# Attention's queries as seven-product units in a stage of their own, ahead of attention, in a hybrid encoder block

## The chip, the cores and the metric

One core of a Trainium2 chip runs the whole layer. The metric is the device time of one execution in microseconds. Engines are named as in the profile: TensorE (PE, with its weight loads PEld), VectorE (DVE), ScalarE (ACT), GpSimd (POOL), and SyncE (SP), whose queue issues nearly all the transfers.

## The reference

One encoder layer on 16 learned meta tokens followed by 1024 tokens of width 1024. `u` is the normed stream; one projection of it feeds everything:

```python
z = u @ w_in
rq, rk, rv, rg, aq, ak, av, ag, gr, ga = _split_in(z)
# retention: 4 heads, keys of 128, values of 256, rotary on rq and rk, scanned forward and backward
o_r = _bidirectional_retention(rq, rk, rv, lg_f, lg_b)[:, META_PAD:]   # then group norm per head
o_r = o_r * ret_nw * silu(rg);            y_r = o_r @ w_rb
# attention: 8 query heads, 2 groups of keys and values, rotary on aq and ak, window of +-128,
# the meta keys always visible, a learned sink logit per head
o_a = _windowed_sink_attention(aq, ak, av, sink)
o_a = o_a * silu(ag);                     y_a = o_a @ w_ab
mix = sigmoid(gr) * y_r + sigmoid(ga) * y_a
return h + _rms_norm(mix @ w_o, post_w)   # meta tokens dropped at the end
```

## The kernel before, in words

**Precision.** Every large product is made from two parts of each operand, a rounded high part (fp32r) and the low rest: `mm3` issues three matmuls, high x high, low x high, high x low. The high part is made by ScalarE (or by GpSimd, `pool_hi`), the low part by VectorE (`dve_lo`, a subtraction). `x`, scaled by the norm's weight and split so, stays in the tiles `big` (two parts of two halves of k); the row factor of the norm is applied behind the products.

**Weights.** `w_in` lies in units of 256 columns: 0 to 3 queries and keys of retention (`U_QK`), 4 to 7 its values, 8 to 11 its gates, 12 and 13 attention's keys and values (`U_AK`, `U_AV`), 14 to 17 its queries (`U_AQ`), 18 to 21 its gates, 22 to 29 the merge gates.

**Order of the work.**

1. Setup: loads, `x` in parts, the first head's queries and keys.
2. Retention, head by head (`retention(h, fill)`): values are projected and the chunks run forward; then a second pass runs the chunks backward. Between its short matmuls `fill` advances a generator of other work: the next head's queries and keys (`gen_qk`) and some early gate products, and for the last head attention's keys (`gen_ak`) and the first two query units (`gen_aq`), 16 steps a chunk.
3. Attention's values (`gen_av`), kept in SBUF as `vah` and `val`.
4. `attention()`: 32 chunks, each of 64 tokens and the four heads of one key group, in three stages (scores and softmax; transposes; values). A chunk's three stages lie apart in time, and between them `fill` advances `works`: the other two query units, then the early gate products. `START` and `FILL` say how much, in units of half a step; a step is one `mm3` of 128x512. `BEGUN` says at which step other things start: fetches, splits, and the sums of `x` (`sum_fetch`, `sum_scale`, `sum_row`), which go to DRAM as `xs`.
5. `steps`, from `run(phases)`: phase "z" (all 16 gate units), "r" and "a" (the two branch projections, 4 units each) and "o" (the output projection).

**Seven products.** A unit in a `Phase` is a product of 256 x 1024 by 1024 x 1024, cut into 2 x 2 blocks and made from seven block products instead of eight, of sums of blocks: operands A11, A12, S4, A22, S1, S2, S3 against B11, B21, B22, T4, T1, T2, T3 (`PROD`). One block product is 12 matmuls of 128x512. `prepare` makes a weight operand's sum and its two parts, `LEAD` = 6 products ahead; `product` issues the matmuls; `combine` adds up in PSUM banks X, Y, Z and in SBUF; `post` finishes an output. T1 to T4 are sums of blocks of `x`. Products that need only plain `x` can be made early (`PRE`, `gen_pre`): they go to DRAM as `e` and are added later.

The query projection, in contrast, is plain: `proj` runs 8 blocks of k, 3 matmuls each, for each of two column halves and two token halves, 96 matmuls a unit (`paq`), and `rope_evac` turns the result from PSUM: three multiplications on VectorE and an addition on GpSimd.

The order in which each engine issues is the program's order as a scheduler arranges it; `tc.issue_after` and `follow` pin some instructions behind others.

Of the kernel before, what the change touches and what calls it, by code (L numbers as in the profile page):

```python
# [14 lines left out]
NM = 16  # L15
T = NM + SEQ
P = 128
# [9 lines left out]
START = 6, 6  # L27
FILL = (((5, 4),) * 1 + ((5, 5),) * 1 + ((6, 4),) * 1 + ((4, 3),) * 1 + ((4, 5),) * 2 + ((4, 7),) * 1 + ((3,
        5),) * 1 + ((6, 4),) * 1 + ((5, 4),) * 1 + ((5, 3),) * 1 + ((2, 4),) * 1 + ((5, 7),) * 1 + ((4, 5),)
        * 1 + ((1, 4),) * 1 + ((6, 1),) * 1 + ((3, 5),) * 1 + ((4, 5),) * 1 + ((4, 4),) * 1 + ((6, 4),) * 1 +  # L30
        ((4, 4),) * 1 + ((4, 3),) * 1 + ((3, 4),) * 1 + ((4, 4),) * 1 + ((4, 2),) * 1 + ((4, 4),) * 1 + ((5,
        4),) * 1 + ((3, 4),) * 1 + ((4, 4),) * 1)
PRE = {u: (2, 3) if u > 4 else (2,) for u in range(2, 14)}
# [11 lines left out]
def block_kernel(ctx: ExitStack, tc: tile.TileContext, xT, x, meta, w_in, w_rb, w_ab, w_out, vecs, dec, sink,  # L45
# [25 lines left out]
    xs_d = [dram.tile([4, P, 2, 512], F32, tag=f"xs{i}", name=f"xs{i}") for i in range(2)]  # L71
# [3 lines left out]
    latest = []  # L75
# [76 lines left out]
    xm = wp.tile([P, KT, 2 * 32], R, tag="xm", bufs=1, name="xm")  # L152
    nc.vector.memset(xm.bitcast(F32), 0.0)

# [25 lines left out]

    ra_stack = ExitStack()
    ra = ra_stack.enter_context(tc.tile_pool(name="ra", bufs=1, reuse_waits="tile"))
    ident = ra.tile([P, P], F32, name="ident")
    cr = ra.tile([P, T], F32, name="cr")
    sr = ra.tile([P, T], F32, name="sr")
# [12 lines left out]
    DT = ra.tile([P, NH, P], F32, tag="DT", bufs=1, name="DT")  # L198
    tabt = ra.tile([P, MW], F32, tag="tab", bufs=1, name="tabt")
    idx = tabt[:, 3 * P:3 * P + 5]  # L200
    warm = ra.tile([P, 1], F32, name="warm")
    dect, neg, na, e, e2, s_, ss, acc, lg = (ra.tile([P, 8], F32, name=n) for n in (
        "dect", "neg", "na", "e", "e2", "s_", "ss", "acc", "lg"))
    ecst, ex = (ra.tile([P, 28], F32, name=n) for n in ("ecst", "ex"))
# [40 lines left out]
    def decay_table(hs):  # L245
        for h in hs:
            t = ra.tile([P, P], F32, tag="rw", bufs=3, name=f"dd{h}")
# [158 lines left out]
    def row_factors(cs):  # L406
# [3 lines left out]
        for c in cs:  # L410
            a, b = cols(c)
            n = b - a
            rw = ra.tile([P, P], F32, tag="rw", bufs=3, name=f"rw{c}")
            nc.scalar.copy(rw[0:n], rcol[0:n, c:c + 1].to_broadcast([n, P]))
            nc.tensor.transpose(t[:, a - base:b - base], rw[0:n], ident[0:n, 0:n])
# [25 lines left out]
    vah = va.tile([P, NB, 256], R, name="vah")  # L441
    vm = va.tile([NM, 2, 256], R, name="vm")
# [4 lines left out]
    rp = r_stack.enter_context(tc.tile_pool(name="rp", bufs=1, reuse_waits="tile"))  # L447

# [16 lines left out]
    pend, masks = [], []  # L465

    def retention(h, fill):
        q, kt = qk[h]
# [9 lines left out]
        vmeta = rp.tile([NM, 256], F32, tag="vmeta", bufs=2, name=f"vmeta{h}")  # L478
# [14 lines left out]
        def stage1(c):  # L493
            n = NM if c == 0 else P
            pv = first.pop(0) if first else projT(wv, c, f"pv{h}_{c}", vmeta)
            vh = rp.tile([P, 256], R, tag="vh", bufs=4, name=f"vh{h}_{c}")
            vl = rp.tile([P, 256], R, tag="vl", bufs=4, name=f"vl{h}_{c}")
# [7 lines left out]
            for d in ("f", "b"):  # L505
# [3 lines left out]
                a = rp.tile([P, P], R, tag="kh" + d, bufs=2, name=f"kh{d}{h}_{c}")  # L509
                b = rp.tile([P, P], R, tag="kl" + d, bufs=2, name=f"kl{d}{h}_{c}")  # L510
# [5 lines left out]
            if c > 0:  # L516
                sd = rp.tile([P, P], F32, tag="sd", bufs=3, name=f"sd{h}_{c}")
                a = rp.tile([P, P], R, tag="sh", bufs=3, name=f"sh{h}_{c}")
                b = rp.tile([P, P], R, tag="sl", bufs=3, name=f"sl{h}_{c}")
# [44 lines left out]
        for c in range(9):  # L564
# [7 lines left out]
            if h == NH - 1 and c == 1:  # L572
                wak.append(load_w(w_in, U_AK))
                masks.append(ra.tile([P, MW], F32, tag="tab", bufs=1, name="mask"))
                nc.sync.dma_start(masks[0], tab[:, 0:MW])
# [10 lines left out]


# [21 lines left out]
        for c in range(NB, 0, -1):  # L609
# [25 lines left out]
            if c < 8:  # L635
                with ExitStack() as behind:
                    for p in pins:
                        behind.enter_context(tc.issue_after(p))
                    fill(KT if h < NH - 1 else 2 * KT)
            if c < NB - 1:  # L640
                finish(c + 2)
        state["n", 1]()
# [17 lines left out]
    aqf, aqs, wq, made = {}, {}, {}, set()  # L660
    aq_d = [dram.tile([4, P, SEQ], F32, tag=f"aq{g}", name=f"aq_d{g}") for g in range(2)]

    def load_q(g, m):

        assert {(2 * g + p, m // 4, e_) for p in range(2) for e_ in range(2)} <= made
        aqf[g, m] = o = aw.tile([P, 4, P], F32, tag="qf", bufs=2, name=f"qf{g}_{m}")
        nc.sync.dma_start(o, aq_d[g][:, :, P * m:P * m + P].rearrange("h p t -> p h t"))

    def split_q(g, m):

        o = aqf.pop((g, m)).rearrange("p e (b t) -> p b e t", b=2)
        h, l = (aw.tile([P, 2, 4, 64], R, tag=f"aq{t}", bufs=2, name=f"aq{t}{g}_{m}") for t in "hl")
# [4 lines left out]
    def fetch_aq(hp):  # L677
        raw = fetch_w(w_in, U_AQ + hp)
        split, wq[hp] = halves_w(U_AQ + hp)
        begun["q", hp] = lambda s: split(raw[s], "apart")  # L680

    def half_w(which, i, s):
        if (which, i, s) in low_w:
            low_w.pop((which, i, s))()
        else:
            low_w[which, i, s] = begun[which, i](s)

    begun, low_w = {}, {}

    def gen_aq(hp, i):  # L690
        if hp not in wq:
            wq[hp] = load_w(w_in, U_AQ + hp)
        a, b = HALVES[i]
        for e_ in range(2):
            t = yield from proj(wq[hp], P * e_, a, b, f"paq{hp}_{i}{e_}")
            o = ra.tile([P, 512], F32, tag="q", bufs=6, name=f"aq{hp}_{i}{e_}")
            with follow(*marks("lo")):
                rope_evac(t, a, b, o, f"aq{hp}_{i}{e_}")
            made.add((hp, i, e_))
            nc.sync.dma_start(aq_d[hp // 2][2 * (hp % 2) + e_, :, 512 * i:512 * i + 512], o)  # L700
            yield

# [3 lines left out]
    ak_d = dram.tile([P, T], F32, tag="ak", name="ak_d")  # L706
    later_k = []

    def load_k():

        later_k.append(aw.tile([P, T], F32, tag="kf", bufs=1, name="kf"))
        nc.sync.dma_start(later_k[0], ak_d)

    def keys(g, i, x, meta=None):

        if not i:
            kT[g] = [ra.tile([P, NB, 144], R, tag="kp", bufs=2, name=f"kT{s}{g}") for s in "hl"]
# [11 lines left out]
    def gen_ak(g, pieces_=range(4)):  # L729
        if not wak:  # L730
            wak.append(load_w(w_in, U_AK))
        for i in pieces_:
# [4 lines left out]
            if g:  # L737
                nc.sync.dma_start(ak_d[:, a:b], o[:, 0:b - a])
            else:
                s = NM if i == 0 else 0  # L740
                keys(g, i, o[:, s:s + 256], None if i else o[:, 0:NM])
# [5 lines left out]
    def sum_fetch(q):  # L747

        k, c = q // 2, slice(256 * (q % 2), 256 * (q % 2) + 256)
        xsum[q] = {}  # L750
        for i in range(2):
            xsum[q][i] = t = xs_tile[q % 2][i](f"xs{i}{q}")
            nc.sync.dma_start(t, xT[4 * i + k, :, NM:T].rearrange("p (j t) -> p j t", j=2)[:, :, c])

    xs_tile = [(lambda n, tag=tag: aw.tile([P, 2, 256], F32, tag="xs", bufs=2, name=n)) for tag in range(2)], [
        lambda n: ra.tile([P, 2, 256], F32, tag="DT", bufs=1, name=n),
        lambda n: wp.tile([P, 2, 256], F32, tag="xm", bufs=1, name=n)]

    def sum_scale(q):

        for i, t in xsum[q].items():
            nc.scalar.activation(t, t, AF.Copy, scale=vec[:, 4 * i + q // 2:4 * i + q // 2 + 1])

    def sum_row(q):

# [890 lines left out]
```

## Time and profile before

| | |
|---|---|
| three runs | 1059.12, 1059.22, 1060.39 us (median 1059.22) |
| profiled execution | 1059.64 us, of which the span from first to last instruction is 1057.8 us |
| granted TensorE clock | 0.998 |
| busy: PE / DVE / ACT / POOL | 98% / 80% / 46% / 20% |
| DMA | 191.67 MB, mean 181 GB/s |
| attention's key projection | 271 to 304 us |
| value projection | 352 to 377 us |
| attention, first scores to last value product | 379 to 564 us |

How to read it: stretches are in microseconds from the span's start. Groups give line, engine, operation, output and inputs by the program's names, shape and count, then busy time, mean length of one in ns, and the engine's idle time just before them with what ended it. Matmuls overlap, so their lengths add up to more than the time they take.

### The profile page before, as it was taken

The numbers are of one execution on the slowest core, as the hardware profiler recorded it, in microseconds if no ns is written. First come the engines' busy times: TensorE is split into PE (matmuls) and PEld (weight loads), VectorE is DVE, ScalarE is ACT, GpSimd is POOL, SyncE is SP. The second block draws the span as 40 slices with busy tenths as digits, with TensorE's granted clock in tenths as the row PEclk, the third lists the DMA queues.
The fourth block names the chain that finished last, engine by engine and source line by source line (L and its number), as shares of the span: only waits on it lengthen the run. The fifth ranks groups of instructions, "written<-read, shape, count | busy, mean of one in ns | idle before, by whom it ended". The sixth has DMA issues, their size and how long they took to land.

```text
span 1057.8 us, 17121 instructions
## 1 busy us (share of the span) xinstructions
PE 1039.7 (98%) x5845; PEld 899.5 (85%) x5845; DVE 850.9 (80%) x1753; ACT 485.9 (46%) x1068; POOL 216.5 (20%) x272
## 2 busy tenths in 40 slices
PE   8999999999999999999999999999999999999996
PEld 7998999989998988978987888777888888787885
DVE  7887788778988458797869988999799799768664
ACT  5541432413411245566667444455466455343442
POOL 3425225325244124322210000000000000111032
PEclk9999999999999999999999999999999999999999
DMA  9412312303123626577759779999925747789365
GB/s 332 160 60 86 106 59 90 125 12 129 51 81 100 189 83 193 165 239 213 209 161 313 216 245 324 305 334 340 373 90 180 256 142 262 196 230 326 91 99 80
DMA packets 110551, 191.67 MB, mean 181 GB/s; under 512 B 11056, under 2 KB 49840, under 8 KB 109632
## 3 DMA queue, kind: packets, MB, share of 16 engines
q1 hardware_dynamic: 106576, 183.49, 52.5%
q0 software_dynamic: 3744, 6.82, 4.4%
q8 instruction: 46, 0.75, 0.3%
q14 instruction: 41, 0.34, 0.1%
q10 hardware_dynamic: 144, 0.27, 0.1%
HBM read 128.67 MB, written 63.18 MB: 181 GB/s over the span
## 4 chain that ended last, share of the span: by engine, by line
PE 81%; DVE 8%; DMA 6%; ACT 2%; issue 2%; SPq 0%; DVEq 0%; POOLq 0%; ACTq 0%
PE bz L80 5%; PE bz L79 5%; PE bz L81 5%; PE pv L81 3%; PE pv L79 3%; PE pv L80 3%; PE paq L80 3%; PE paq L79 3%; PE paq L81 3%; PE bo L80 2%; PE bo L79 2%; PE bo L81 2%; PE ba L80 2%; PE ba L79 2%; PE ba L81 2%
## 5 line engine op out<-in xcount | busy, mean ns | idle before, releaser
L1242 POOL DMA_DIRECT2D mx_d<-c1a x4 | 3.7, 917 | 394.8 <-DVE c1a L1233 391.5
L79 PE MATMUL bz<-T,lhz 128*128 128x512 f32 x192 | 75.6, 395 | 0.5 <-DVE u2z L1026 0.4
L81 PE MATMUL bz<-T,lhz 128*128 128x512 f32 x192 | 75.8, 395 | 0.0
L80 PE MATMUL bz<-T,llz 128*128 128x512 f32 x192 | 75.7, 395 | 0.0
L81 PE MATMUL pv<-wl,big 128*128 128x256 f32 x256 | 73.1, 285 | 0.0
L79 PE MATMUL pv<-wh,big 128*128 128x256 f32 x256 | 72.8, 285 | 0.0
L80 PE MATMUL pv<-wh,big 128*128 128x256 f32 x256 | 72.7, 284 | 0.0
L79 PE MATMUL bz<-big,lhz 128*128 128x512 f32 x172 | 67.8, 397 | 2.0 <-ACT lhz L941 2.0
L80 PE MATMUL bz<-big,llz 128*128 128x512 f32 x172 | 68.2, 396 | 0.0
L81 PE MATMUL bz<-big,lhz 128*128 128x512 f32 x172 | 67.7, 394 | 0.0
L1413 POOL TENSOR_SCALAR p<-p,den 128x352 f32<-128x352 f32 (+2 forms) x60 | 38.9, 661 | 96.7 <-DVE den L1406 86.2
L1403 ACT ACTIVATE p<-raw,nm 128x353 f32<-128x353 f32 (+2 forms) x64 | 36.1, 566 | 43.8 <-DVE nm L1400 41.8
L79 PE MATMUL paq<-big,wh 128*128 128x512 f32 x128 | 51.9, 405 | 0.0
L80 PE MATMUL paq<-big,wl 128*128 128x512 f32 x128 | 50.8, 396 | 0.0
L81 PE MATMUL paq<-big,wh 128*128 128x512 f32 x128 | 50.4, 394 | 0.0
L599 ACT ACTIVATE ost<-to,rnw 128x128 f32<-128x128 f32 x64 | 19.8, 363 | 65.0 <-PE to L594 50.1
L81 PEld LDWEIGHTS pv<-wl,big 128*128 128x128 f32 x256 | 48.3, 189 | 0.4
L79 PEld LDWEIGHTS pv<-wh,big 128*128 128x128 f32 x256 | 48.3, 189 | 0.2
L80 PEld LDWEIGHTS pv<-wh,big 128*128 128x128 f32 x256 | 48.2, 188 | 0.0
L79 PEld LDWEIGHTS bz<-T,lhz 128*128 128x128 f32 x192 | 36.1, 188 | 9.5 <-DVE u2z L1026 1.2
L81 PEld LDWEIGHTS bz<-T,lhz 128*128 128x128 f32 x192 | 36.2, 188 | 8.5
L80 PEld LDWEIGHTS bz<-T,llz 128*128 128x128 f32 x192 | 36.2, 188 | 8.3
(612 smaller groups left out, 3567.6 us busy)
## 6 DMA issues: line engine op xcount, KB each, us to landing
wrz<-in_w_in_dram SPq DMA_DIRECT2D x32, 512.0 KB, 6.2
wr<-in_w_in_dram SPq DMA_DIRECT2D x27, 512.0 KB, 4.0
e<-e SPq DMA_DIRECT2D x42, 256.0 KB, 4.3
we<-in_w_in_dram SPq DMA_DIRECT2D x18, 512.0 KB, 4.1
tg<-tg_d SPq DMA_DIRECT2D x32, 256.0 KB, 4.9
T<-preT SPq DMA_DIRECT2D x6, 1024.0 KB, 7.8
xt<-in_x_dram SPq DMA_DIRECT2D x8, 512.0 KB, 8.8
oTr_d<-ost SPq DMA_DIRECT2D x16, 256.0 KB, 2.2
```

The lines of the kernel that those rows point to most:

```text
L79: nc.tensor.matmul(o, ah, bh, start=first, stop=False, **kw)
L80: nc.tensor.matmul(o, al, bh, start=False, stop=False, **kw)
L81: latest[:] = [nc.tensor.matmul(o, ah, bl, start=False, stop=last, **kw).ins]
L599: nc.scalar.activation(ost[0][:, e_, w0:w0 + P], to[:, P * e_:P * e_ + P], AF.Copy, scale=rnw[:, 2 * h + e_:2 * h + e_ + 1])
L1242: nc.gpsimd.dma_start(d, to, accum_op=ALU.add)
L1403: last["exp"] = nc.scalar.activation(p[:, 0:1 + wid], raw[e_][:, 0:1 + wid], AF.Exp, scale=-1.0, bias=nm_[:, e_:e_ + 1], accum_out=den[:, ...
L1413: nc.gpsimd.tensor_scalar(pt[e_][:, 0:wid], pt[e_][:, 0:wid], den[:, e_:e_ + 1], 1.0, op0=ALU.mult, op1=ALU.mult)
```

## The change: what it does

- **Queries as units of seven products.** The four query units (16 to 19 in the new numbering of gates) leave `gen_aq` and run in a phase of their own, "y", with the gate units 0 to 3 (`FIRST`): eight units, two at a time, after the value projection and before attention. A query's output is turned by `query_post` and stored to `aq_d`. The operands of two units share tiles of the weight pool (`paired`), and operand sums are made in place.
- **Sums of x earlier.** Rows of `x` are loaded and scaled in the last head's second pass and summed during the value projection (`x_load`, `x_scale`, `x_sums`). T1 stays in `big`; T2, T3 and T4 are split for the new phase, written to DRAM in both parts (`t_store`) and read back for phase "z" without a split (`get_sum`).
- **The last head's second pass** advances 9 steps a chunk (`LAST`), the two key groups alone. Both go through DRAM (`ak_d`), as do the values (`av_d`, `vm_d`): attention loads them when it begins.
- **Early products.** Units 4 to 7 and 10 to 15 (`LATER`) now have three, 2, 3 and 5; units 8 and 9 (`EARLY`) none. Product 2 of six units is made in retention (`BORDER`), of the others during phase "y"; 3 and 5 fill attention. Sum S2 goes through DRAM (`s2_d`).
- **Phase "z"** has units 8 and 9 and the ten of `LATER`, these with four products each, 1, 6, 7 and 4. As B21, B22 and T1 are not needed there by then, their refill for the next phase starts 48 products ahead (`REFILL`).
- The sums of `w_out` for phase "o" (`pre_load`, `pre_split`) move from phase "z" into phase "y" and attention.
- Tables (`VALUES_AT`, `FIRST_AT`, `BEGUN`) say at which step each of these is issued. The host lays the units of `w_in` out in blocks.

```diff
-START = 6, 6
-FILL = (((5, 4),) * 1 + ((5, 5),) * 1 + ((6, 4),) * 1 + ((4, 3),) * 1 + ((4, 5),) * 2 + ((4, 7),) * 1 + ((3,
...
-PRE = {u: (2, 3) if u > 4 else (2,) for u in range(2, 14)}
+START = 4, 12
+FILL = ((2, 2),) * 1 + ((2, 1),) * 1 + ((2, 3),) * 2 + ((4, 3),) * 1 + ((2, 3),) * 6 + ((2, 4),) * 1 + ...
+EARLY = 8, 9
+LATER = 4, 10, 5, 11, 6, 12, 7, 13, 14, 15
+PRE = {u: (2, 3, 5) for u in LATER}
+BORDER = 12, 0, 12
+LAST = 9
+REFILL = -48, 5, 5
+LEADS = 2, 4, 6
+VALUES_AT = ((-1, "w1", "s0", "s1"), (1, "l2"), (4, "w0"), (6, "c2"), (8, "n6", "s2", "pT2.0.1.2"),
+             (16, "f0", "l3"), (17, "f1", "f2"), (20, "c3", "z"), (21, "s3", "f3"), (22, "pT2.3"))
+FIRST_AT = ((1, "k6"), (2, "pT3"), (6, "pT4"), (7, "m4"), (12, "tT3"), (13, "x0"), (14, "tT2", "tT4"),
+            (16, "y0.0"), (17, "y0.1"), (18, "y0.2"), (19, "y0.3", "x1"), (23, "y1.0"), (24, "m4", "y1.1"),
+            (26, "y1.2"), (27, "y1.3", "n8"), (28, "x2"), (31, "y2.0", "k8"), (33, "y2.1"), (35, "y2.2"),
+            (37, "y2.3"), (44, "A0"), (47, "m4"), (49, "r", "F4"), (51, "S4", "P4", "A1"),
+            (52, "L4", "F10", "A2"), (53, "A3"), (54, "m4", "S10", "P10", "L10", "F5"))
...
-                    fill(KT if h < NH - 1 else 2 * KT)
+                    fill(KT if h < NH - 1 else LAST)
             if c < NB - 1:
                 finish(c + 2)
+            if h == NH - 1:
+                for f, k in {6: [(x_load, 0)], 5: [(x_load, 1)], 4: [(x_scale, 0)], 3: [(x_scale, 1)]}.get(c, ()):
+                    f(k)
...
-        fill, drain = filler([gen_qk(h + 1), pieces(pre, (8, 8, 4)[h])] if h < 3 else [gen_ak(0), gen_ak(1), gen_aq(0, 0), gen_aq(0, 1), gen_aq(1, 0), gen_aq(1, 1)])
+        fill, drain = filler([gen_qk(h + 1), pieces(pre, BORDER[h])] if h < 3 else [gen_ak(0), gen_ak(1)])
...
         def split(self, u, p, src):
-            h, l = (lp.tile([P, 4, P], R, tag=t, bufs=LEAD, name=f"{t}{self.nm}{u}_{p}") for t in ("lh", "ll"))
+            if self.paired:
+                n, e_ = self.at[u]
+                if not e_:
+                    self.pair[n, p] = [wp.tile([P, 4, 256], R, tag=f"w{x}", bufs=4, name=f"w{x}{self.nm}{n}_{p}")
+                                       for x in "hl"]
+                h, l = (part(t, e_) for t in (self.pair.pop if e_ else self.pair.get)((n, p)))
+            else:
+                h, l = (lp.tile([P, 4, P], R, tag=t, bufs=LEAD, name=f"{t}{self.nm}{u}_{p}") for t in ("lh", "ll"))
             nc.scalar.copy(h, src)
             dve_lo(l, src, h)
...
     def get_sum(n):
-        for k in range(4):
-            t = stage(f"x{n}{k}", n in ("T2", "T3"))
-            i, j = next(o for m, o, *_ in SUMS if m == n)
-            nc.sync.dma_start(t, xs_d[i][k][:, j])
-            split_b(n, k, t)
+        for v, d in zip(B[n], t_d[n]):
+            nc.sync.dma_start(v.bitcast(F32), d)
...
+    def query_post(u, i, j, o, to=None):
+        s, to = half[j], o if to is None else to
+        m2 = spare[0].tile([P, 512], F32, tag="m2", bufs=2, name=f"m2_aq{u}{i}{j}")
+        nc.vector.tensor_tensor(m2[64:128], o[0:64], sr[0:64, s], mul)
+        nc.vector.tensor_tensor(m2[0:64], o[64:128], sr[64:128, s], mul)
+        nc.vector.tensor_tensor(to, o, cr[:, s], mul)
+        nc.gpsimd.tensor_tensor(to, to, m2, add)
+        made.add((u, j, i))
+        nc.sync.dma_start(aq_d[u // 2][2 * (u % 2) + i, :, 512 * j:512 * j + 512], to)
...
+    FIRST = 0, 1, 16, 17, 18, 19, 2, 3
+    first_seq = sequence(FIRST)
+    first_seq[:14] = [(u, p) for u in (0, 1) for p in (1, 2)] + [(u, p) for p in (5, 6, 7, 3, 4) for u in (0, 1)]
+    first_seq[-14:] = [(u, p) for p in (1, 5, 6, 7, 4, 2, 3) for u in FIRST[-2:]]
+    first_phase = Phase("y", first_seq, w_loader(w_in, gates), first_post, first_fetch, paired=True)
+    steps = run([(Phase("z", sequence(EARLY + LATER, (1, 3, 2, 5, 6, 7, 4)), pre_loader, z_post, z_fetch,
+                        early=EARLY, pre=PRE),
...
-        works = hooked([(gen_aq(2, 0), 2), (gen_aq(3, 0), 2), (gen_aq(2, 1), 2), (gen_aq(3, 1), 2), (pre, 2)], BEGUN)
+        works = hooked([(fifths(), 2)], BEGUN)
...
+        nc.sync.dma_start(vah.bitcast(F32), av_d[0])
+        nc.sync.dma_start(val.bitcast(F32), av_d[1])
         edge_values(0, 0)
         edge_values(0, 1)
...
+    jobs = dict(l=x_load, c=x_scale, s=x_sums, p=x_parts, f=x_first, t=t_store, m=more, n=second_fetch,
+                k=second_parts, x=lambda k: pre_load(k, act_src(w_out)), y=pre_split, A=ready, F=pre_fetch, S=pre_sums,
+                P=pre_parts, L=pre_low, z=lambda _: next(first), w=first_weights, r=lambda _: first_phase.raw.clear())
...
+    for n, _ in enumerate(gen_av()):
+        with tc.high_priority(400):
+            do(table, n)
...
+    e_from[0] = p2
+    free[:] = ["pj"] * 3 + ["p1"] * 2 + ["p3"]
+    table = at(FIRST_AT)
+    for n, _ in enumerate(first):
+        do(table, n)
...
+    at1, at2, atv = (a_stack.enter_context(tc.tile_pool(name=n, bufs=1, reuse_waits="tile"))
+                     for n in ("at1", "at2", "atv"))
+    vah, val = (atv.tile([P, NB, 256], R, name=n) for n in ("vah", "val"))
```

In a table, a letter is a job of `jobs`, and what follows it its arguments: "y1.2" makes `pre_split(1, 2)`, "m4" four steps of the early products, "A0" to "A3" ready attention's inputs.

More of the change, by code (lines that the diff above doesn't have):

```diff
@@ new lines, in second_fetch, with second_parts @@
+    def second_fetch(n):
+        pool, tag, bufs = (lp, "w2", 1) if lp else (keep, "wr", 2)
+        fetched_w[n, 2] = t = pool.tile([P, 4, 256], F32, tag=tag, bufs=bufs, name=f"w2_{n}")
+        for i, u in enumerate(LATER[n:n + 2]):
+            nc.sync.dma_start(part(t, i), part(w_in[gates[u], :, 4:8, :], 0))
+    def second_parts(n):
+        h, l, low = parts_of(fetched_w.pop((n, 2)), f"w2_{n}")
+        low()
+        for i, u in enumerate(LATER[n:n + 2]):
+            parts[u, 2] = part(h, i), part(l, i)
@@ L866, in pieces @@
             yield next(gen)
[L868 to L872 removed]
+    pre = seconds()
     softmax, last = [], {}
@@ L1082, in sequence @@
     def sequence(n, first=ORDER):
+        if not isinstance(n, int):
+            return [(u, p) for i in range(0, len(n), 2) for p in (ORDER if i else first) for u in n[i:i + 2]]
         if n % 2:
@@ new lines, in block_kernel, with first_weights @@
+    first = run([(first_phase, None)], {}, lead=lambda i: LEADS[(i > 0) + (i > 2)])
+    def first_weights(u):
+        for n in ("A11", "A12"):
+            first_phase.block(u, n)
+    jobs = dict(l=x_load, c=x_scale, s=x_sums, p=x_parts, f=x_first, t=t_store, m=more, n=second_fetch, k=second_parts, x=lambda k: pre_load(k, act_src(w_out)), y=pre_split, A=ready, F=pre_fetch, S=pre_sums, P=pre_parts,
+                L=pre_low, z=lambda _: next(first), w=first_weights, r=lambda _: first_phase.raw.clear())
```

651 lines of the change are left out of this document (391 added, 260 removed).

## The prediction

> **What bounds the kernel now.** I read the page's head and busy times first, then its chain.
>
> ```profile
> span 1057.8 us, 17121 instructions
> PE 1039.7 (98%) x5845; PEld 899.5 (85%) x5845; DVE 850.9 (80%) x1753; ACT 485.9 (46%) x1068; POOL 216.5 (20%) x272
> PE 81%; DVE 8%; DMA 6%; ACT 2%; issue 2%; SPq 0%; DVEq 0%; POOLq 0%; ACTq 0%
> ```
>
> TensorE sets the time: busy 98%, 81% of the chain. So the first question is how many products TensorE has to issue, the second who makes it wait. Next I read TensorE's timeline inside the query projection, because busy time counts overlapping matmuls.
>
> ```profile
> 332.66 0.40 PE L79 MATMUL paq<-big,wh 128*128 128x512 f32 x1
> 332.89 0.40 PE L80 MATMUL paq<-big,wl 128*128 128x512 f32 x1
> ...
> 334.05 0.39 PE L79 MATMUL paq<-big,wh 128*128 128x512 f32 x1
> ```
>
> A record is 0.39 to 0.40 us long, but the next starts after 0.232 us (seven rows, the middle left out: 1.39 us over six steps). This step, not the record, is the price of one 128x512 matmul: a product of a sequence (4 blocks of k, 3 matmuls each) costs 12 x 0.232 = 2.78 us.
>
> The busy times by stage show who is close behind. Columns: stretch, length, then busy us and instructions of PE, weight load, DVE, ACT, POOL; granted clock, DMA share, GB/s.
>
> ```profile
> 352.50:377.20 24.70, 24.70 (x210) 24.51 (x208) 8.85 (x18) 8.13 (x17) 2.33 (x1) 1.00 0.56 171
> 440.00:500.00 60.00, 57.74 (x346) 50.81 (x345) 48.62 (x117) 38.18 (x97) 15.57 (x22) 1.00 0.69 211
> 500.00:551.00 51.00, 50.15 (x314) 45.19 (x313) 35.99 (x90) 35.87 (x94) 11.86 (x18) 1.00 0.62 182
> 577.00:640.00 63.00, 63.00 (x273) 51.04 (x272) 58.20 (x97) 31.24 (x56) 0.00 (x0) 1.00 0.76 245
> 640.00:760.00 120.00, 117.55 (x503) 94.16 (x502) 105.31 (x173) 61.43 (x106) 0.00 (x0) 1.00 0.98 337
> ```
>
> Here 352.5 to 377.2 is the value projection, the next two are the later part of attention, the last two lie in the gates. In attention TensorE loses 2.26 + 0.85 = 3.1 us, in the full gate stretch 2.45 us where the DMA share is 0.98. The gates live with VectorE 58.2 of 63 us busy and lose nothing: a VectorE near 92% is no bound by itself, as operands are split six products ahead.
>
> **What the change removes.** The groups by line count the query products, and one wait:
>
> ```profile
> L79 PE MATMUL paq<-big,wh 128*128 128x512 f32 x128 | 51.9, 405 | 0.0
> L80 PE MATMUL paq<-big,wl 128*128 128x512 f32 x128 | 50.8, 396 | 0.0
> L81 PE MATMUL paq<-big,wh 128*128 128x512 f32 x128 | 50.4, 394 | 0.0
> L80 PE MATMUL pe<-big,wel 128*128 128x512 f32 x84 | 33.6, 400 | 3.1 <-DVE wel L95 3.1
> ```
>
> The four query units take 384 matmuls; seven products each are 4 x 84 = 336. The gates keep 16 x 84 = 1344 in all, early products included. So 48 matmuls go, all of them on the path: 48 x 0.232 = **-11.1 us**. (By record length it would be 19 us, which the timeline forbids.) The Trainium skill's page "TensorE: Matmul & The Clock Gate", Back-to-back issue gap, gives about 0.131 us sustained for 512 columns, by which the gain would be an estimated 6.3 us; the trace's 0.232 us decides.
>
> **What it adds in the eight-unit stage.** TensorE: 8 x 84 matmuls and 48 of early products beside them. VectorE's prices:
>
> ```profile
> 783.87 0.68 DVE L95 TENSOR_TENSOR llz<-wrz,lhz 128x512 fp32r<-128x512 f32 x1
> 784.47 0.68 DVE L1111 TENSOR_TENSOR z<-z,z 128x512 f32<-128x512 f32 x1
> 785.07 0.68 DVE L95 TENSOR_TENSOR llz<-stz14S,lhz 128x512 fp32r<-128x512 f32 x1
> ...
> 457.90 0.69 DVE L192 TENSOR_TENSOR m_aq<-paq,sr 64x512 f32<-64x512 f32 x1
> 458.60 0.69 DVE L193 TENSOR_TENSOR m_aq<-paq,sr 64x512 f32<-64x512 f32 x1
> ```
>
> Start to start, a 128x512 costs 0.60 us and a rotary half 0.70 us. A query unit needs 7 low splits, 4 operand sums and 3 combines (14 x 0.60 = 8.4 us) and four rotated outputs at 2 x 0.70 + 0.60 = 2.0 us: 16.4 us beside 7 x 2.78 = 19.5 us of TensorE. A gate unit swaps the rotation for two operations an output: 13.2 us. During the four query units (65.6 us) the tables also put twelve splits of w_out (a sum and a low part each, 14.4 us) and one weight low part of two such widths (1.2 us): 81.2 us against TensorE's 28 products and one early product, 29 x 2.78 = 80.6 us. VectorE is full there, and GpSimd adds the rotated halves at the same time:
>
> ```profile
> 312.24 1.29 POOL L194 TENSOR_TENSOR aq<-m_aq,m_aq 128x512 f32<-128x512 f32 x1 [1.42 <-DVE m_aq L193]
> ...
> 312.59 1.22 DVE L95 TENSOR_TENSOR Slb<-Sb,Shb 128x256 fp32r<-128x256 f32 x1
> ...
> 447.70 1.54 POOL L194 TENSOR_TENSOR aq<-m_aq,m_aq 128x512 f32<-128x512 f32 x1 [6.20 <-issue]
> ...
> 448.11 0.69 DVE L95 TENSOR_TENSOR pal<-pt,pah 128x512 fp32r<-128x512 f32 x1
> ...
> L95 DVE TENSOR_TENSOR Slf<-Sf,Shf 128x256 fp32r<-128x256 f32 x32 | 15.1, 470 | 0.8 <-POOL Shf L92 0.6
> ```
>
> Beside such an addition the subtraction of two SBUF tiles took 1.22 us where its like takes 0.47, and ended with it; the one that reads PSUM (pal) was not held. So each of the 16 additions costs VectorE about 0.75 us (12 us), at most its own 1.29 us (20.6 us), at least nothing where PSUM reads fall beside it. The Trainium skill's page "SBUF — State Buffer", Who interferes with whom, states this as a rule: an instruction of VectorE with two SBUF inputs and one of GpSimd that reads SBUF exclude each other; the trace agrees (1.22 against 0.47 us).
>
> VectorE then falls 81.2 + 12 - 80.6 = 12.6 us behind. The weight halves have four pair buffers: one in use, one taken by the early products' parts for long stretches, two ahead, worth 4 products or 11.1 us. About 1.5 us reach TensorE; with the shorter lead at the start and the reordered last pair I take **+3** (0 to +20.6, all of it if nothing is ahead). ScalarE at 46% has room for its 7 high splits a unit.
>
> **Changeovers.** Keys and values now go through DRAM: behind the last outputs of the new stage the SP queue waits for that stage's tiles, then loads two 1 MB value tiles; the edge loads and next queries queue behind them.
>
> ```profile
> 379.11 0.26 PE L79 MATMUL ps<-kTh,aqh 128*128 128x208 f32 x1
> ...
> 393.09 0.28 PE L79 MATMUL po<-pah,vah 128*128 128x256 f32 x1
> ...
> 564.17 0.28 PE L81 MATMUL po<-pbl,v 80*128 80x256 f32 x1
> ...
> 578.19 0.39 PE L79 MATMUL bz<-T,lhz 128*128 128x512 f32 x1
> ...
> T<-preT SPq DMA_DIRECT2D x6, 1024.0 KB, 7.8
> ```
>
> The first value product comes 14.0 us after the first scores. Between them the tables now put 19 units of filler, not 25, at half a step of three matmuls (0.35 us) each, and 4 ahead of the first scores: 14.0 - 2.1 + 1.4 = 13.3 us from the end of the new stage. The loads take 7.8 us if they run together and 15.6 us one after the other, behind the last store: 0 to 4 us late. Into the gates, T2, T3 and T4 are six 1 MB loads, once attention's tiles are free; the first is needed 14.0 us after attention's last product, the others 5.6 us apart, and at 6.2 us a pair (2.1 MB at the 337 GB/s above) they land by about 8, 14 and 20 us: in time, unless other loads sit between. In their own stage the gates then move some 45 MB in 54 x 2.78 = 150 us, 300 GB/s of 337. I take **+2** (0 to +8).
>
> **Attention and gates.** Attention loses half of the rope work and all the sums of x; 80 steps of filler remain of 128. Of its 3.1 us of waits, all in front of an early product's low part, I give back **-2** (-3.1 to +2: eight such parts are made there, as before). The last head's second pass has 9 filler steps per chunk instead of 16; the heads before it live with 8. Sums of x move into the value projection, where VectorE is busy 8.85 of 24.7 us. Gates: **0** (-2.5 to +4).
>
> Sum: -11.1 + 3 + 2 - 2 = -8.1 us. The profiled execution took 1059.6 us (span 1057.8), 0.4 above the median of 1059.22, so 1051.1: I say **1051**.
>
> **Rivals.** (1) VectorE becomes the bound in the query units: GpSimd holds it for all 16 additions in full and the operand lead does not cover it, because a product's split is queued behind the rotation of the one before. Then 20.6 us arrive: 1059.2 - 11.1 + 20.6 + 2 - 2 = 1069. It decides against the change from 11 us of waits on. For it: 81.2 of 80.6 us before any hold; against it: the lead, and PSUM readers in between. (2) The changeovers cost their 8 us and the attention gains nothing: 1059.2 - 11.1 + 3 + 8 = 1059, no change. (3) Everything hides and attention's and the gates' waits go: 1059.2 - 11.1 - 3.1 - 2.5 = 1043. That the count of products does not fall I exclude: the sequences spell out each of them.
>
> **How the numbers follow.** Forecast 54%, its own range 1044 to 1057; (1) 28%, with all that a full VectorE may bring; (2) 8%; (3) 10%. A measurement tells about 0.2% (2.1 us) from no change. Faster is forecast and (3): 64%; same is (2): 8%; slower is (1): 28%. The range, 1043 to 1067, takes in (3), (2) and most of (1).
>
> **What would show it.** Right: 48 fewer 128x512 matmuls at an unchanged step of 0.232 us; queries' products named by the new sequence; in its middle VectorE busy in all of a window, with low splits of 1.2 us beside GpSimd's additions, and only some us of TensorE's idle time ended by VectorE; attention's stretch shorter with less waiting. Wrong: a product of that stage regularly late by half a microsecond or more, the first value product waiting for its DMA, or the first T2 product waiting for a load.

## The result

The changed kernel takes **1068.14 us** (median of six runs, 1067.16 to 1071.10), the kernel before beside it 1059.81 us: a ratio of **1.0077, 95% interval 1.0059 to 1.0094**. It is slower, where 1051 us and "faster" were forecast, and 1 us outside the range. The profiled execution took 1067.16 us. From the head of the page of the changed kernel, with its busy times and its chain:

```profile
span 1065.4 us, 17204 instructions
PE 1033.8 (97%) x5797; PEld 893.1 (84%) x5797; DVE 866.9 (81%) x1750; ACT 510.5 (48%) x1116; POOL 214.7 (20%) x268
PE 80%; DVE 9%; DMA 7%; issue 2%; ACT 1%; POOL 1%; SPq 0%; DVEq 0%; POOLq 0%; ACTq 0%
```

TensorE's records fell from 5845 to 5797: the 48 matmuls are gone. Yet the span grew by 7.6 us, so TensorE lost about 19 us elsewhere. The busy times by stage say where to look (columns as in the prediction):

```profile
336.00:516.00 180.00, 171.38 (x737) 137.46 (x736) 157.04 (x235) 71.62 (x131) 27.45 (x20) 0.99 0.65 227
516.00:560.00 44.00, 35.47 (x193) 29.94 (x192) 32.61 (x79) 25.66 (x62) 8.62 (x14) 0.92 0.76 253
560.00:664.00 104.00, 103.16 (x663) 93.65 (x661) 80.85 (x215) 76.53 (x208) 29.37 (x46) 1.00 0.66 208
664.00:825.00 161.00, 159.73 (x702) 129.36 (x702) 141.14 (x233) 97.93 (x185) 0.00 (x0) 1.00 0.95 336
```

The first is the new eight-unit stage, the second the entry into attention, then the rest of attention and the gates. TensorE has no work for 8.6 us of the first and 8.5 us of the second, where its clock is also down to 0.92; the gates, at a DMA share of 0.95, lose little. TensorE's own waits in the first two stretches (what it waited for: us in total, times, longest):

```profile
PE by L94 <- DVE c5y L1448: 4.4, 1, 4.4
PE by L95 <- DVE wly L110: 4.2, 4, 2.1
...
PE pt L1547 <- POOL p L1536: 2.7, 2, 2.4
PE pe L95 <- DVE w_10l L110: 2.4, 1, 2.4
PE ps L94 <- DVE nm L1523: 1.3, 1, 1.3
PE ps L95 <- DVE aql L110: 1.1, 1, 1.1
```

All of the first two and three of the last four name VectorE. What VectorE did ahead of the first of them and of the longest stands in the timeline, with rows of GpSimd, TensorE and ScalarE between:

```profile
430.89 0.68 DVE L1033 TENSOR_TENSOR wry<-wry,wry 128x512 f32<-128x512 f32 x1
431.06 1.64 POOL L1449 TENSOR_TENSOR c5y<-c5y,m_aq 128x512 f32<-128x512 f32 x1 [6.10 <-DVE c5y L1448]
431.49 1.76 DVE L1033 TENSOR_TENSOR wry<-wry 128x512 f32<-128x512 f32 x1
433.18 1.28 DVE L110 TENSOR_TENSOR wly<-wry,why 128x512 fp32r<-128x512 f32 x2
433.91 0.50 PE L95 MATMUL by<-T2q,wly 128*128 128x512 f32 x1 [2.06 <-DVE wly L110]
...
486.21 2.95 DVE L110 TENSOR_TENSOR wly<-wry,why 128x512 fp32r<-128x512 f32 x3
486.42 1.59 POOL L1449 TENSOR_TENSOR u2y<-u2y,m_aq 128x512 f32<-128x512 f32 x1 [1.29 <-DVE u2y L1448]
486.67 0.40 PE L94 MATMUL by<-big,why 128*128 128x512 f32 x1
490.13 0.58 ACT L1105 COPY u2y<-by 128x512 f32<-128x512 f32 x1 [5.17 <-DMA aq_d<-u2y]
490.60 0.69 DVE L1448 TENSOR_TENSOR c5y<-by,cr 128x512 f32<-128x512 f32 x1
491.44 0.76 PE L94 MATMUL by<-big,why 128*128 128x512 f32 x1 [4.38 <-DVE c5y L1448]
492.96 0.63 PE L94 MATMUL by<-big,why 128*128 128x512 f32 x1
```

At 431.49 an operation of two SBUF tiles takes 1.76 us instead of 0.68 beside GpSimd's addition and ends half a microsecond after it; the low part that TensorE needs comes right behind. At 486.67 TensorE waits for no operand: its next product needs a PSUM bank, which is free only when VectorE has turned the output in it (line 1448), and that stands in VectorE's queue behind three low parts, one of them held. Behind this wait of 4.4 us the next matmuls are 0.42 to 0.56 us apart (1.52 us for the first three), not 0.232. ScalarE had a bank to empty as well, and stood 5.17 us until the store of the tile that it writes over had landed, a store that stands behind GpSimd's addition at 486.42. It was done at 490.71, 0.6 us ahead of the rotation, so this wait ends with VectorE; the delayed store lies close behind.

To compare stages between kernels I sum, over all of TensorE's records, by how much the start-to-start time exceeds the median of that shape. This account takes in waits, slow steps and everything between:

| us lost by TensorE | up to the stage | query stage | 32 us behind it | rest of attention | gates to the end | sum |
|---|---|---|---|---|---|---|
| before (query and value projections; first 40 us of attention) | 9.2 | 0.6 | 1.1 | 7.1 | 6.7 | 24.6 |
| changed | 11.2 | 11.7 | 11.3 | 7.2 | 2.9 | 44.4 |

The stage costs 11.1 us more, the entry 10.2; the gates give back 3.8. The stretch ahead of the stage loses 2.0 us more, in pieces of less than a microsecond, which no run takes apart. Together 19.8, less 11.1 for the 48 matmuls, is 8.7 us beside the 7.5 us between the two profiled executions.

### The profile page after: what moved, and what is told of

Its sections match the earlier page's. It is cut to its first block, busy times and chain, and to the rows that moved or that the text cites. A ratio compares the mean times of both kernels' runs of the same rounds, so it can differ in the third digit from the quotient of the medians.

```text
span 1065.4 us, 17204 instructions
## 1 busy us (share of the span) xinstructions
PE 1033.8 (97%) x5797; PEld 893.1 (84%) x5797; DVE 866.9 (81%) x1750; ACT 510.5 (48%) x1116; POOL 214.7 (20%) x268
## 4 chain that ended last, share of the span: by engine, by line
PE 80%; DVE 9%; DMA 7%; issue 2%; ACT 1%; POOL 1%; SPq 0%; DVEq 0%; POOLq 0%; ACTq 0%
PE bz L95 5%; PE bz L94 5%; PE bz L96 5%; PE pv L95 3%; PE pv L94 3%; PE pv L96 3%; PE bo L95 2%; PE bo L94 2%; PE br L95 2%; PE bo L96 2%; PE br L94 2%; PE br L96 2%; PE by L95 2%; PE by L96 2%; PE by L94 2%
## 5 line engine op out<-in xcount | busy, mean ns | idle before, releaser
L1011 ACT CAST why<-wry 128x512 fp32r<-128x512 f32 x56 | 32.9, 620 | 57.9 <-DVE wry L1033 33.0
L94 PE MATMUL bz<-T,lhz 128*128 128x512 f32 x144 | 56.8, 395 | 0.0
L96 PE MATMUL bz<-T,lhz 128*128 128x512 f32 x144 | 56.8, 394 | 0.0
L95 PE MATMUL bz<-T,llz 128*128 128x512 f32 x144 | 56.8, 394 | 0.0
L94 PE MATMUL by<-big,why 128*128 128x512 f32 x128 | 51.0, 400 | 4.4 <-DVE c5y L1448 4.4
L95 PE MATMUL by<-big,wly 128*128 128x512 f32 x128 | 51.3, 401 | 0.0
L96 PE MATMUL by<-big,why 128*128 128x512 f32 x128 | 50.8, 397 | 0.0
L110 DVE TENSOR_TENSOR wly<-wry,why 128x512 fp32r<-128x512 f32 x56 | 43.7, 802 | 6.3 <-ACT why L1011 6.0
L1523 DVE CUSTOM_DVE_ANT_0 raw<-ps,mask,nsink 128x352 f32<-128x352 f32 (+2 forms) x64 | 33.2, 548 | 3.0 <-ACT p L1526 1.6
L595 ACT ACTIVATE op<-pa,rcol 128x256 f32<-128x256 f32 x32 | 15.2, 476 | 42.0 <-PE pa L96 41.6
L687 POOL TENSOR_TENSOR rs<-rs,mhalf 128x1 f32<-128x1 f32 x32 | 23.3, 729 | 52.8 <-DVE rs L686 49.6
L94 PEld LDWEIGHTS by<-big,why 128*128 128x128 f32 x128 | 24.4, 191 | 10.7 <-ACT u2y L1105 4.8
## 6 DMA issues: line engine op xcount, KB each, us to landing
T<-tT SPq DMA_DIRECT2D x6, 1024.0 KB, 10.8
```

The costliest lines, as they stand in the source:

```text
L94: nc.tensor.matmul(o, ah, bh, start=first, stop=False, **kw)
L95: nc.tensor.matmul(o, al, bh, start=False, stop=False, **kw)
L96: latest[:] = [nc.tensor.matmul(o, ah, bl, start=False, stop=last, **kw).ins]
L110: return nc.vector.tensor_tensor(o, i, hi.bitcast(F32), ALU.subtract).ins
L595: nc.scalar.activation(o, pa[:, 0:256], AF.Copy, scale=rcol[:, c:c + 1])
L687: nc.gpsimd.tensor_tensor(rs, rs, mhalf[:, 0:1], ALU.pow)
```

## The experiments

**Theory A**: GpSimd's 16 additions of rotated halves hold VectorE, and in a stage where VectorE has no slack that reaches TensorE. **Theory C**: the entry into attention has a price of its own, set by VectorE's queue there (loads, sums and parts of the next early products between the last outputs and the first scores). **Theory D**, formed later: the first softmax waits for a store. Theory B, that the moved work alone overfills VectorE, and other rivals stand in the expectations. Ratios are to the kernel before, run beside each; the losses are TensorE's, as in the table above. e1, e9 and e13 leave the additions out, so their queries lack the sums: they price the additions and replace no kernel.

### The additions: none, on VectorE, or twice

```diff
 query_post():
-        nc.gpsimd.tensor_tensor(to, to, m2, add)      # e1: left out
+        nc.vector.tensor_tensor(to, to, m2, add)      # e2: on VectorE
+        nc.gpsimd.tensor_tensor(to, to, m2, add)      # e5: as it was, and behind it
+        nc.gpsimd.tensor_tensor(m2, m2, m2, add)      #     a second one of the same size
```

> The 16 additions of GpSimd in the query stage are left out (the queries stay half rotated); everything else stays. Theory A, GpSimd's additions hold VectorE (15.3 us in the changed kernel's trace) and this is what TensorE waits for: most of the 11 us of waits in the stage and a part of the 11 us at attention's entry go, 1055 us (1052 to 1059). Theory B, VectorE is over-full by the moved work itself and the hold is minor: 1065 or more. Theory C, the loss is at attention's entry, from a weight fetch that blocks VectorE's queue and from the softmax's start: 1066 to 1068.

> The 16 additions run on VectorE instead of GpSimd. A: 16 x 0.60 = 9.6 us of VectorE's own work in place of 15.3 us of hold, so 3 to 8 us less, 1062 us (1059 to 1065), and no operation of VectorE in the stage takes over 1 us. B: 9.6 us more on a full engine, 1072 or more. C: 1067 to 1069.

> Behind each of the 16 additions GpSimd makes a second one of the same size, on a tile that nobody reads afterwards. A: the hold doubles, 10 to 16 us more, 1080 us (1077 to 1086). B and C: GpSimd is idle there otherwise and nobody waits for the second, 1068 to 1070.

| | us | ratio, 95% interval | lost in the stage | 32 us behind it |
|---|---|---|---|---|
| e1, none | 1058.60 | 0.9983 (0.9971 to 0.9995) | 0.4 | 13.5 |
| e2, on VectorE | 1063.68 | 1.0026 (1.0007 to 1.0045) | 0.8 | 18.5 |
| changed, on GpSimd | 1068.14 | 1.0077 (1.0059 to 1.0094) | 11.7 | 11.3 |
| e5, twice on GpSimd | 1078.91 | 1.0179 (1.0157 to 1.0202) | 16.2 | 18.3 |

The dose answers: one set of additions on GpSimd costs 10.0 us (1.0077 less 0.9983, of 1060), a second set 10.8 us, of which the stage shows 4.5 and the entry 7.0. Theory B asked for 1065 us or more without the additions and falls. On VectorE, 16 x 0.60 = 9.6 us more of its time leave one wait of 0.2 us in the stage: it is the hold that hurts there, more than the work. Nor is it that others wait for GpSimd's sums: no wait of VectorE in the stage ends with one of the additions, in the changed kernel or in e5. The stores behind the sums do hold ScalarE, but in e2 as well (2.7 us at 446.07, 3.4 us at 492.35), where TensorE loses next to nothing. Theory A stands. But neither e1 nor e2 gains what the stage gives up: at the entry they lose 2.2 and 7.2 us more than the changed kernel. TensorE's waits there, of e1, then of e2:

```profile
PE pe L94 <- ACT w_10h L790: 5.2, 1, 5.2
PE ps L94 <- DVE nm L1522: 2.1, 2, 1.6
```

```profile
PE pe L94 <- ACT w_10h L790: 9.5, 1, 9.5
PE pe L94 <- ACT w_5h L790: 3.2, 1, 3.2
```

A stage that ends sooner arrives sooner at weights that are not there yet: the loads for units 10 and 5 wait for the buffers of unit 4, which the next edit tests for unit 10.

### Less work for VectorE in the query units

```diff
-FIRST_AT: "x0" "x1" "x2" and "y0.0" to "y2.3"    (loads and twelve sums and splits of w_out)
+BEGUN: the three loads at steps 1, 14, 27 of attention's filler, the splits 7 to 10 steps behind each
```

> The twelve splits of w_out (14.4 us of VectorE) leave the query units and are made in attention. A and B both: the waits in the stage fall by most of 11 us, and attention takes up to 3 us more: 1058 us (1055 to 1063); under A operations of VectorE beside the additions still take 1.7 us but nobody waits for them. C: the entry's 11 us stay, 1066 to 1070.

It took 1079.02 us, 1.018 (1.0158 to 1.0202): a miss. The stage does lose only 3.7 us instead of 11.7, so room on VectorE hides the hold too. But the rest of attention loses 25.7 instead of 7.2 us. VectorE's own waits in attention say how (rows of its view of waits):

```profile
DVE we L859 <- DMA we<-in_w_in_dram: 6.3, 2, 5.4
...
DVE we L859 <- DMA v<-vm_d: 5.8, 1, 5.8
DVE raw L1522 <- ACT p L1525: 5.8, 1, 5.8
DVE we L859 <- DMA preT<-wT11h: 4.8, 1, 4.8
```

VectorE stands at the head of its queue for a weight load (line 859), and transposes and softmax behind it wait as well. The move put the loads and stores of w_out on the queue of transfers that these weights come by, and VectorE's queue passes the delay on. That it is the transfers, not the 14.4 us of work, I read from these rows; no run separates the two.

### An earlier load for unit 10

```diff
 pre_fetch(u):
-    fetched_w[u] = [keep.tile(..., tag="wr", bufs=2, ...)
+    fetched_w[u] = [(lp if u == 10 else keep).tile(..., tag="wr", bufs=2, ...)
 FIRST_AT:
-    (49, "r", "F4"), ... (52, "L4", "F10", "A2"), ... (54, "m4", "S10", "P10", "L10", "F5")
+    (49, "r", "F4", "F10"), ... (52, "L4", "F5", "A2"), ... (54, "m4", "S10", "P10", "L10")
```

> As the run with the 16 additions on VectorE (1063.68 us), and unit 10's two loads of weights go into the two buffers that the query stage has given up and are issued three steps earlier, unit 5's load follows in the buffers of unit 4. Theory C (once the additions no longer hold VectorE, what is left of the loss is the chain load - sum - split of units 10 and 5 at attention's entry, which waits for buffers): the waits of 9.6 us for w_10h and 3.4 us for w_5h go, 1063.7 - 9 to 13 = 1051 to 1055, the stretch from 500 to 540 us has under 9 us of waits where it had 19.6. Rival (the entry costs what it costs because attention's first scores, exponentials and table load have nothing before them): the wait moves to another tile and the time stays at 1061 to 1065.

> The changed kernel with the same earlier load of unit 10's weights and the additions left on GpSimd. Theory A (the additions' hold is a price of its own): the 11.4 us of waits inside the query stage stay, and of the entry's 11 us at most the 2.5 us for w_10l and its followers go: 1064 to 1068, 9 us or more above the run with VectorE's additions and the earlier load. Theory C alone (the loss is the load chain only, the waits in the stage would be made up later): 1055 to 1059.

> As the run without the 16 additions (1058.6 us; their sums are left out of the queries), with the earlier load of unit 10's weights. If the prices of hold and entry are separate: 1058.6 less the 5.4 us wait for w_10h and some of the 2.8 us of shorter waits beside it, 1051 to 1054, at or a little under the run with VectorE's additions and the earlier load. If the entry is bound by attention's own first steps: 1057 to 1060.

| | us | ratio, 95% interval | stage | behind it |
|---|---|---|---|---|
| e7, VectorE adds | 1060.58 | 1.0010 (0.9996 to 1.0024) | 3.6 | 12.1 |
| e8, GpSimd adds | 1066.45 | 1.0054 (1.0029 to 1.0080) | 13.1 | 9.6 |
| e9, no additions | 1052.60 | 0.9932 (0.9910 to 0.9954) | 0.4 | 9.6 |

The waits for w_10h and w_5h go. With no additions this is worth 5.4 us (0.9983 to 0.9932), so C is a price beside A's, and e8 against e9, 13 us apart, shows A once more. By the ratios e8 lies only 4.7 us above e7, though, where 9 or more were expected: with GpSimd's additions the earlier load is worth 2.4 us and with VectorE's 1.7, both within the intervals. For e7 that misses the 9 to 13 us of theory C and comes near the rival's answer: the wait moves to the first score reduction. VectorE's and SP's rows there in e7:

```profile
514.68 0.38 SPq L1334 DMA_DIRECT2D oTr_d<-c5y  x1
515.36 0.69 DVE L1333 TENSOR_TENSOR u2y<-u2y,v 128x512 f32<-128x512 f32 x1 [0.70 <-ACT u2y L1330]
520.76 0.44 DVE L1523 CUSTOM_DVE_ANT_0 raw<-ps,mask,nsink 128x208 f32<-128x208 f32 x1 [4.71 <-DMA oTr_d<-c5y]
```

The tiles of attention's row maxima lie on the memory of the query stage's last output (`c5y`). Its store, issued at 514.68 behind other loads, landed at 520.58 by the trace, and the reduction starts 0.18 us later.

### A gap in memory, and additions by the transfer

```diff
 e10, e11, e13:
-    at1, at2, atv = ...
+    at1, gap, at2, atv = ...
+    gap.tile([P, 512], F32, name="gap")              # attention's maxima and exponentials lie 2 KB further
 e10, e12 (query_post):
-        nc.gpsimd.tensor_tensor(to, to, m2, add)
-        nc.sync.dma_start(aq_d[...], to)
+        nc.sync.dma_start(aq_d[...], m2)
+        nc.gpsimd.dma_start(aq_d[...], to, accum_op=add)
```

> As the run with VectorE's additions and the earlier load of unit 10 (1060.6 us), with the gap of 2 KB alone added. Theory D (attention's first softmax waits for the last output's store because its tiles lie on that output's memory): the 5.6 us wait for the first score reduction goes, 1055 to 1057. Rival (the reduction waited for its place in VectorE's queue or for the mask): 1060 to 1061.

> The changed kernel with the 16 additions made by the transfers, nothing else. Theory A: as the run that left the additions out, 1057 to 1061, with no waits inside the query stage. Rival (issuing on GpSimd holds VectorE, or the accumulating transfers hold the outputs): 1064 to 1070, with the stage's waits still there.

> Three edits on the changed kernel: the 16 additions are made by the transfer (the second half of the rotation is stored, the first is added to it in memory by a transfer that GpSimd issues), so neither GpSimd nor VectorE adds; unit 10's weights are loaded earlier; and a gap of 2 KB moves attention's row maxima and exponentials off the memory of the query stage's last output, whose store the first score reduction waited for (its store landed at 520.6 us and the reduction began at 520.8 in the run with VectorE's additions and the earlier load). Theories A and C together: the run without additions and with the earlier load gave 1052.6; less the 5 us wait for the first reduction, of which the products that follow take some time over: 1047 to 1051, faster than the kernel before. Rival (the accumulating transfers hold the outputs, or their issue on GpSimd holds VectorE as the additions did): waits come back in the stage, 1056 to 1064.

| | us | ratio, 95% interval | stage | behind it |
|---|---|---|---|---|
| e11, VectorE adds, load, gap | 1058.85 | 0.9982 (0.9969 to 0.9995) | 4.4 | 7.8 |
| e12, transfer adds | 1064.35 | 1.0048 (1.0022 to 1.0073) | 7.2 | 16.4 |
| e10, transfer adds, load, gap | 1058.69 | 0.9989 (0.9974 to 1.0003) | 7.4 | 14.3 |

In e11 the reduction no longer waits for the store (D holds: it starts at 516.07, right behind VectorE's work, where it stood 4.71 us in e7), but the time falls by 3 us by the ratios and the expectation of 1055 is missed. What is left of TensorE's waits in e11 is in its timeline:

```profile
508.07 0.50 PE L95 MATMUL pe<-big,w_4l 128*128 128x512 f32 x1 [2.78 <-DVE w_4l L110]
513.01 0.50 PE L95 MATMUL pe<-big,w_10l 128*128 128x512 f32 x1 [1.21 <-DVE w_10l L110]
516.56 0.40 PE L94 MATMUL ps<-kTh,aqh 128*128 128x288 f32 x1 [0.73 <-DVE nm L1523]
520.06 0.33 PE L1547 MATMUL pt<-ident,p 128*128 128x128 f32 x1 [2.44 <-POOL p L1536]
```

and VectorE is busy for 19.35 of the 20.1 us from 496.4 to 516.5:

```profile
496.40:516.50 20.10, 15.13 (x65) 11.18 (x64) 19.35 (x35) 9.31 (x16) 0.00 (x0) 1.00 0.85 291
```

The last outputs, sums and parts for two units, keys and queries for attention all fall into this stretch. TensorE has two early products against it, 24 matmuls or 5.6 us.

The additions by transfer fell short of their expectation. (The profiled executions of e10 and e12 took 1062.4 and 1067.6 us, both some 3.5 us above their medians, so their losses are a little high.) The rival has it, by a row of ScalarE's waits between 430 and 450 us in e12:

```profile
ACT u2y L1105 <- DMA aq_d<-u2y: 8.3, 2, 6.0
```

ScalarE is to write the next output into the tile that the accumulating transfer was issued from; that transfer, issued at 437.02, landed at 444.87, and ScalarE began at 444.89. The bank that ScalarE should empty stays full, and one of TensorE's two waits of the stage, 2.3 us, ends with that write. The other, 2.5 us, ends with a rotation on VectorE; what delayed that one stays open.

### The gap without additions, and a later sum

```diff
 e13 = e9 and the gap
 e14 = e11 and
-    (51, "S4", "P4", "A1"), (52, "L4", "F5", "A2"), (53, "A3")
+    (51, "A1"), (52, "S4", "P4", "A2"), (53, "L4", "F5", "A3")
```

> As the run without the 16 additions and with the earlier load (1052.6 us; the sums are left out of the queries), and the gap of 2 KB. If the wait for the last output's store is a price of its own (theory D, from the pair of runs with VectorE's additions, which differ by 1.7 us where their first wait of 5.6 us became one of 0.9 and one of 2.6): 1049 to 1051.5. Rival (the gap's gain in the other pair was the scatter of two medians): 1052 to 1053.5. The expectation of 1047 to 1051 for the accumulating transfers missed for waits inside the stage; with no additions at all they are absent here if they came from those transfers.

> As the run with VectorE's additions, the earlier load of unit 10 and the gap (1058.85 us), with unit 4's sums, its split and unit 5's load one step later. In that run VectorE stood 1.7 us at the first of those sums for its load, ahead of the query stage's last products of the rotation and gating. Theory C (VectorE's queue sets the entry): the 1.7 us idle goes, 1057 to 1058.5. Rival (the split of unit 4 is what TensorE waits for, and it comes later still): 1059 to 1061, the wait for w_4l growing from 2.9 us.

e13 took 1052.75 us, 0.9930 (0.9908 to 0.9952): the same as e9, as the rival has it, so the 3 us between e7 and e11 cannot be put down to the gap as a fixed price. The wait for the reduction fell from 4.9 to 3.0 us, the one for the first transposes rose from 1.1 to 2.6. D's wait is real but not the last one: in e13 the table load (1.28 us, at 512.78) and the exponentials come behind it. e14 took 1058.29 us, **0.9979 (0.9966 to 0.9992)**. Within its interval that is e11. The edit did not do what it was meant to: VectorE's order over the border is the same in both traces, and its idle time ahead of unit 4's first sum is still there (first e11, then e14):

```profile
496.45 0.69 DVE L860 TENSOR_TENSOR we<-we,we 128x512 f32<-128x512 f32 x1 [1.69 <-DMA we<-in_w_in_dram]
497.29 0.69 DVE L860 TENSOR_TENSOR we<-we,we 128x512 f32<-128x512 f32 x1 [1.87 <-DMA we<-in_w_in_dram]
```

So the wait for w_4l, 2.8 us as before, tells nothing of what those 1.7 us cost. e11 and e14 are the versions that beat both kernels: some 2 us faster than before, 10 us faster than the change.

## Why the prediction was wrong, point by point

**-11.1 for the matmuls: right.** 5845 to 5797 records, and the step stayed 0.232 us.

**+3 for the stage: the first step that failed; it measured +11.1.** Of the 11.7 us lost there 8.6 are waits and 1.4 slow steps behind the longest. Three parts of the working went wrong.

- *The hold.* It was put at 0.75 us an addition, 12 us. In the trace VectorE's instructions beside the 16 additions are longer than the median of their shape by 15.3 us in all, 0.96 each: every one of the 16 lay beside a held instruction, the rotations' multiplications too where ScalarE had copied their input to SBUF. Put into the prediction's own sum, that is 81.2 + 15.3 - 80.6 - 11.1 = 4.8 us, an estimate of less than half of what was lost; the rest lies with the cushion and the clock. The group of the low parts shows a share of it, 802 ns against the 0.68 us of an undisturbed one:

```profile
L110 DVE TENSOR_TENSOR wly<-wry,why 128x512 fp32r<-128x512 f32 x56 | 43.7, 802 | 6.3 <-ACT why L1011 6.0
```

- *The cushion.* Operands made ahead were counted as 11.1 us of cover, and the same cover was then set against all that VectorE fell behind. The lead does cover some of it: e2's 9.6 us of additional work left 0.8 us of loss. But VectorE issues in the program's order, and with VectorE full (19.77 of 20 us in 420 to 440) the low parts stand behind rotations and the rotations behind low parts. Four waits, 4.2 us, end with a low part, so the lead had run out there. The longest, 4.4 us, was for a bank, and there a lead in operands covers nothing. The rows (in the second, VectorE idles only from 496.2 us on, for a load):

```profile
420.00:440.00 20.00, 17.93 (x78) 14.12 (x77) 19.77 (x28) 8.81 (x15) 4.94 (x3) 1.00 0.45 157
480.00:500.00 20.00, 15.07 (x59) 11.54 (x58) 15.92 (x20) 6.01 (x11) 4.80 (x3) 0.91 0.33 105
```

- *The clock.* The prediction priced a wait at its length. The second row, with the 4.4 us wait in it, shows a granted clock of 0.91.

Rival (1) named this mechanism, its place and a split queued behind a rotation, and gave it 28%. That its 1069 us came within 1 us is luck: it let 20.6 us of hold reach TensorE in the stage, where 11.1 did, and had 2 us for the changeovers, where the entry took 10.2.

**+2 for the changeovers, -2 for attention: the second step that failed, +10.2 at the entry and +0.1 in the rest of attention.** The working looked at the loads of the two value tiles and the first value product. They did land in time; no wait of TensorE names them. What it did not follow is VectorE's queue over the same border. The weights of units 4, 10 and 5 are loaded, summed and split there, and VectorE stood 6.3 us for the first of these loads. TensorE was still fed then (busy in all of 496 to 516.5 us); the delay reaches it at 522.44, when the low part for unit 10 comes late:

```profile
502.51 0.69 DVE L860 TENSOR_TENSOR we<-we,we 128x512 f32<-128x512 f32 x1 [6.30 <-DMA we<-in_w_in_dram]
521.17 1.22 DVE L110 TENSOR_TENSOR w_10l<-we,w_10h 128x1024 fp32r<-128x1024 f32 x1
522.44 0.50 PE L95 MATMUL pe<-big,w_10l 128*128 128x512 f32 x1 [2.39 <-DVE w_10l L110]
526.57 1.28 ACT L1526 ACT_TABLE_LOAD   x1
530.07 0.47 PE L1547 MATMUL pt<-ident,p 128*128 128x128 f32 x1 [2.42 <-POOL p L1536]
531.94 0.63 PE L95 MATMUL pe<-big,w_4l 128*128 128x512 f32 x1
532.37 0.63 PE L96 MATMUL pe<-big,w_4h 128*128 128x512 f32 x1
```

Then the first exponential has a table load of 1.28 us ahead of it, and the matmuls behind run at a slow clock (0.92 over 516 to 560). In the kernel before, the border into attention cost little: the account there is 1.1 us for the first 40 us. The additions' part of the loss and the entry's part are not simply added: e1, without additions, still loses 13.5 us at the entry, 5.2 of it in the wait for weights that it now reaches too soon. The earlier load takes some of this away, but no run in the tables gets the entry under 7.8 us. That the rest is VectorE's queue and the softmax's start is read from the rows and not shown by a run. e9, with neither additions nor late weights, takes 0.9932 of the kernel before, against 0.992 forecast; but it loses 0.4 us in the stage and 9.6 at the entry, so it comes near the forecast with other terms.

**Gates, 0: better.** They lost 6.7 us before and 2.9 after, -3.8, beyond the -2.5 that was allowed; no run asks why. That their loads of T2 to T4 come in time was right; no wait names them.

**The signs to look for** were the right ones: low parts of over 1.2 us beside additions, a full VectorE in the middle, products late by more than half a microsecond. The last was named as the sign of being wrong, and it came.

## What to carry to other kernels

When an engine is at 100% of a stage on paper, do not take a lead in operands for cover of all that it falls behind: ask for each waiting instruction what stands ahead of it in its engine's queue, and count PSUM banks that wait to be read as well as operands that wait to be made. Where an engine is full, work beside it that holds it up is expensive: 16 additions "on an idle engine" cost 10 us here, and 4.6 us on the busy one. A stage that is made shorter meets the loads behind it sooner; look at the border next, and at whose memory the next stage's first tiles take over.

## What the hardware showed that I had not expected

**The hold works both ways.** Twelve of GpSimd's 16 additions took 1.59 to 1.74 us (two stand in the rows above), the other four 1.29 to 1.30: both engines lose. The twelve began while VectorE was at an instruction with two SBUF inputs, the four while it read PSUM or stood; beside a long addition VectorE lost 1.01 us on average, beside a short one 0.80. The Trainium skill's page "SBUF — State Buffer", Who interferes with whom, states that an instruction of VectorE with two SBUF inputs contends with one of GpSimd that reads SBUF. The trace agrees with it and puts the price at 0.96 us of VectorE for each addition.

**A wait of 4.4 us costs more than 4.4 us.** After the 4.38 us wait six steps were 0.42 to 0.56 us long; after the 2.06 us wait one was 0.34 and the rest 0.23. The Trainium skill's page "TensorE: Matmul & The Clock Gate", Part 1, says that about 3.4 us of idling halves the clock, for about as long again; the two waits of this trace lie on either side of that, and the slow stretch lasted 2.8 us. The length of one wait does not decide it here, though: the wait of 2.42 us that ends at 530.07, behind another of 1.33 us that ends at 526.59, has slow steps behind it too (0.43 us from 531.94 to 532.37, in the last rows shown above).

**An accumulating transfer is no free adder.** It took the work off both engines, but in e12 ScalarE waited up to 6.0 us for its source tile, and that came back as a wait of TensorE. A plain store does this too, less often: in the changed kernel ScalarE stood 5.17 us for one, once.
